# A two-layer attention trunk on one core: the v and gate projections by seven quarter products, and token-major output projections

## The chip, the cores and the metric

The kernel runs on one core of a Trainium2 chip. The metric is the device time of one launch in microseconds (us). The engines are named as in the profile: PE (TensorE, matmuls), PEld (its weight loads), DVE (VectorE), ACT (ScalarE), POOL (GpSimd), SP (SyncE, which issues the DMAs here).

## The reference, cut to what matters

There are 512 tokens of 1024 features and two layers. Both token mixers of a layer read the same normalised input; A has 16 heads of 64 with three dilated patterns, B has 8 differential heads.

```
hdn = rms_norm(x, norm_w)
u = hdn @ w_in                       # 1024 x 10240
qa, ka, va, za, qb, kb, vb, zb, ga, gb = split_cols(u)      # 1024 columns each
ya = dilated_mixture(rope(qa), rope(ka), va) * silu(za)
yb = rms_norm(diff_attention(rope(qb), rope(kb), vb, lam), subln_w) * (1 - lam_init) * silu(zb)
merged = sigmoid(ga) * (ya @ w_proj_a) + sigmoid(gb) * (yb @ w_proj_b)
x = x + merged @ w_out               # after both layers: rms_norm(x, final_norm_w)
```

## The kernel before, in words

**Precision.** Every projection is done as three matmuls of rounded parts: each operand is split into a high part and the rest, and high·high, high·low and low·high are added up in PSUM. The weights come from DRAM in float32 tiles of 128x1024 (`raw`), and for each ACT writes the high part `whi` (L84) and DVE the rest `wlo` (L85).

**Chunks.** A projection of 1024 columns is cut into chunks. `proj_T` makes 256 columns by 512 tokens, feature-major: 48 matmuls of 128x512, weights stationary (L164 to L166). `proj_V` makes 512 tokens by 256 columns, token-major: 96 matmuls of 128x256, the input stationary (L216 to L218). q with k, z, the gates, pa and pb are T chunks, as is layer 0's output projection; v and layer 1's output projection are V chunks.

**Windows.** After a first z, qk and v chunk a layer goes through 17 windows: 8 for the head pairs of branch A, 8 for the heads of branch B and one more. `run` puts the main steps (the chunks' matmuls) and the side steps (a head's scores, softmax, transposes and products with v) of a window in turn. The windows' chunks are qk of the next head, v or z in turn, pa in windows 9 to 12 and the gates in 15 and 16; pb and the output projection follow. `WINDOWS` and `chunk_order` hold that order. A scheduler then fixes one order of instructions for each engine, in which each engine works; buffers of one pool (`blk`, 27 of 4 KB a partition; `tmp`; `wpool` with 3 each of raw, whi and wlo) are taken in turn.

**One head.** The scores `s(layer, branch, head)` go to PSUM; DVE takes the row maximum (L314), ACT the exponential (L315). In branch B, DVE joins the two softmaxes (L408 to L414), PE transposes them to `t` (L332), ACT and DVE split that to `pt` (L333, L334), PE multiplies with v to `o` (L424), and the output is normed (L431 to L443), turned (`ot`, L448), multiplied with the gate path and split to `yb` (L451 to L455). q and k get their rotation on evacuation: a shuffle (L237), products on DVE and POOL (L239, L240), a sum (L241), the split (L248), and DMAs into `qx` and `kx`.

**Input.** `h_block` splits a feature block of x, and `sq_block` squares it on ACT; POOL adds the squares up, and `rstd_cols` sums over the features by 16 matmuls with ones (`ps_ss`, L140). Of the last layer's residual, PE turns x1 to token-major by transposes (`xt`, L564).

Of the kernel before, what the change touches and what calls it, by code (L numbers as in the profile page):

```python
# [12 lines left out]
OP = mybir.AluOpType  # L13
# [19 lines left out]
def trunk_kernel(ctx: ExitStack, tc: tile.TileContext, x, win, wpa, wpb, wout, norm_w, subln_w, final_w, lams,  # L33
                 negb, rope, ident_in, out):
# [3 lines left out]
    blk = ctx.enter_context(tc.tile_pool(name="blk", bufs=27))  # L38
# [22 lines left out]
    halves = [(w, layer, i, h) for layer in range(DEPTH) for w, i in chunk_order() for h in range(2)]  # L61

    def w_src(entry):
        w, layer, i, h = entry
        return {"in": win, "pa": wpa, "pb": wpb, "out": wout}[w][layer, i, h]

    raw, whi, wlo = {}, {}, {}
    n_dma = [0]
    n_split = [0]

    def dma_to(i):
        while n_dma[0] <= min(i, len(halves) - 1):
# [5 lines left out]
    def split_to(i):
        while n_split[0] <= min(i, len(halves) - 1):
            j = n_split[0]  # L80
            dma_to(j)
            whi[j] = wpool.tile([P, 4, 256], F32R, tag="whi", name=f"whi{j}")
            wlo[j] = wpool.tile([P, 4, 256], F32R, tag="wlo", name=f"wlo{j}")
            nc.scalar.activation(whi[j], raw[j], AF.Copy)  # L84
            nc.vector.tensor_tensor(wlo[j], raw.pop(j), bits(whi[j]), OP.subtract)  # L85
            n_split[0] += 1
            dma_to(j + 3)
# [24 lines left out]
    def h_block(layer, m, xt):  # L112

        h = b4(f"h{layer}_{m}")
        nc.scalar.activation(h[:, 0], xt, AF.Copy, scale=nw[:, layer, m:m + 1])
        nc.vector.scalar_tensor_tensor(h[:, 1], xt, nw[:, layer, m:m + 1], bits(h[:, 0]), OP.mult, OP.subtract)  # L116
        st_["hnew"][m] = h

    def sq_block(m, xt):

        s = t2(f"sq{m}")
        nc.scalar.activation(s, xt, AF.Square)  # L122
        if m == 0:
# [9 lines left out]

    def rstd_cols():

        ps = pst.tile([P, T], F32, tag="t", name="ps_ss")
        for n, sq in enumerate((st_["acc"], st_["sq7"])):
            for tb in range(4):
                c = 4 * n + tb
                nc.tensor.matmul(ps[:, c:c + 1], sq[:, tb * P:(tb + 1) * P], ones[:, 0:1], start=True, stop=True)  # L140
# [19 lines left out]
    def mm3(ps, hb, wi, kk, c0, first, last):  # L160

        w_h = whi[wi][:, kk, c0:c0 + P]
        w_l = wlo[wi][:, kk, c0:c0 + P]
        nc.tensor.matmul(ps, w_h, hb[:, 0], start=first, stop=False)  # L164
        nc.tensor.matmul(ps, w_h, hb[:, 1], start=False, stop=False)  # L165
        nc.tensor.matmul(ps, w_l, hb[:, 0], start=False, stop=last)  # L166

    chunk_no = [0]

    def proj_T(rhs, evac, first=False):  # L170
# [635 lines left out]
```

## Time and profile before

| | |
|---|---|
| time of three runs | 1409.91 us median (1409.31 to 1410.14) |
| time of the profiled execution, its span | 1411.3 us, 1409.5 us |
| mean granted TensorE clock | 0.994 of full speed |
| busy: PE, PEld | 1384.4 us (98%), 1197.9 us (85%) |
| busy: DVE, ACT, POOL | 914.5 us (65%), 718.2 us (51%), 317.9 us (23%) |
| DMA queue of the kernel | 180.73 MB, 44.6% of 16 engines' span |

Busy time is the union of an engine's instructions; the matmuls overlap in it, so their cost is read from start to start. The profile's 40 slices show PE at nine tenths or more in all but the first two and the last, so that the end moves with PE's work and with PE's waits.

### The profile page before, as it was taken

The page shows a single profiled execution, that of the slowest core. Times are in us where ns is not written, and L with a number is a line of the kernel's source. Part 1 is how long each engine was busy: PE and PEld are TensorE (multiplying, and loading weights), DVE is VectorE, ACT ScalarE, POOL GpSimd, SP SyncE. Part 2 cuts the span into 40 slices and gives each one's busy share as a digit, 9 for nine tenths or more (in the row PEclk, how much of TensorE's full clock was granted, in tenths as well). Part 3 has the DMA queues.
Part 4 walks back from the last instruction along what each step waited for, and adds up shares of the span by engine and source line. Part 5 has one row for each costly group of instructions (what it writes and reads, how often), then busy time and mean ns, then how long its engine had stood idle before and what let it go on. Part 6 is the DMA issues. An engine that isn't in the chain of part 4 may idle for free.

```text
span 1409.5 us, 21036 instructions
## 1 busy us (share of the span) xinstructions
PE 1384.4 (98%) x7592; PEld 1197.9 (85%) x7592; DVE 914.5 (65%) x1836; ACT 718.2 (51%) x1402; POOL 317.9 (23%) x251
## 2 busy tenths in 40 slices
PE   7899999999999999999989999999999999999998
PEld 6798888988888988888878988989888989888898
DVE  6677777775567775345546777777755778653554
ACT  4456565654455666333434565655544656653333
POOL 3353444400011111110213444444001111111000
PEclk9999999999999999999999999999999999999999
DMA  6464554445535453332544554445535344533521
GB/s 213 125 165 116 140 134 120 120 116 153 151 116 138 121 150 120 105 105 93 186 136 117 138 139 120 120 109 137 144 119 164 105 135 115 148 112 106 163 84 67
DMA packets 67559, 182.07 MB, mean 129 GB/s; under 512 B 9984, under 2 KB 10112, under 8 KB 67456
## 3 DMA queue, kind: packets, MB, share of 16 engines
q1 hardware_dynamic: 67456, 180.73, 44.6%
q8 instruction: 60, 0.98, 0.3%
q14 instruction: 43, 0.35, 0.1%
HBM read 121.97 MB, written 8.39 MB: 92 GB/s over the span
## 4 chain that ended last, share of the span: by engine, by line
PE 95%; DVE 2%; DMA 1%; issue 1%; ACT 1%; SPq 0%; POOL 0%; POOLq 0%; ACTq 0%
PE pj L164 22%; PE pj L165 21%; PE pj L166 21%; PE pv L216 5%; PE pv L218 5%; PE pv L217 5%; DMA x<-x_d 0%; DMA kx(1, 0, 0)0_6921<-hl(1, 0, 0)1_6918 0%; DVE h L116 0%; DVE wlo L85 0%; DMA kx(1, 0, 1)1_7204<-hl(1, 0, 1)1_7197 0%; PE xt L564 0%; PE ps_ss L140 0%; DMA kx(0, 0, 0)0_364<-hl(0, 0, 0)1_361 0%; SPq L232 0%
## 5 line engine op out<-in xcount | busy, mean ns | idle before, releaser
L164 PE MATMUL pj<-h,whi 128*128 128x512 f32 x1024 | 410.0, 402 | 5.9 <-DVE whi L621 5.9
L165 PE MATMUL pj<-h,whi 128*128 128x512 f32 x1024 | 403.2, 394 | 1.2 <-DVE h L116 1.1
L166 PE MATMUL pj<-h,wlo 128*128 128x512 f32 x1024 | 403.0, 395 | 0.1
L85 DVE TENSOR_TENSOR wlo<-raw,whi 128x1024 fp32r<-128x1024 f32 x207 | 276.0, 1334 | 111.7 <-ACT whi L84 108.5
L84 ACT ACTIVATE whi<-raw 128x1024 fp32r<-128x1024 f32 x207 | 218.5, 1056 | 175.9 <-PE pj L165 100.2
L166 PEld LDWEIGHTS pj<-h,wlo 128*128 128x128 f32 x1024 | 192.8, 188 | 41.7 <-DVE wlo L85 0.5
L164 PEld LDWEIGHTS pj<-h,whi 128*128 128x128 f32 x1024 | 193.2, 189 | 39.4 <-issue 5.9
L165 PEld LDWEIGHTS pj<-h,whi 128*128 128x128 f32 x1024 | 193.2, 189 | 34.9 <-DVE h L116 2.9
L216 PE MATMUL pv<-whi,h 128*128 128x256 f32 x512 | 148.5, 290 | 0.0
L218 PE MATMUL pv<-whi,h 128*128 128x256 f32 x512 | 146.5, 286 | 0.0
L217 PE MATMUL pv<-wlo,h 128*128 128x256 f32 x512 | 146.4, 286 | 0.0
L217 PEld LDWEIGHTS pv<-wlo,h 128*128 128x128 f32 x512 | 99.5, 194 | 1.1
L216 PEld LDWEIGHTS pv<-whi,h 128*128 128x128 f32 x512 | 99.4, 194 | 1.0
L218 PEld LDWEIGHTS pv<-whi,h 128*128 128x128 f32 x512 | 99.3, 194 | 0.1
L517 POOL TENSOR_TENSOR g<-g,pr 128x512 f32<-128x512 f32 x16 | 23.7, 1482 | 138.0 <-ACT g L516 105.4
L514 DVE TENSOR_TENSOR g<-pj,rb 128x512 f32<-128x512 f32 x32 | 22.1, 689 | 25.6 <-PE pj L166 25.4
L126 POOL TENSOR_TENSOR sq<-sq,sq 128x512 f32<-128x512 f32 x12 | 18.9, 1575 | 86.4 <-ACT sq L122 86.1
L217 PE MATMUL pv<-wlo,mg 128*128 128x256 f32 x128 | 35.7, 283 | 0.0
L218 PE MATMUL pv<-whi,mg 128*128 128x256 f32 x128 | 35.7, 283 | 0.0
L216 PE MATMUL pv<-whi,mg 128*128 128x256 f32 x128 | 35.4, 283 | 0.0
L525 DVE TENSOR_TENSOR g<-pj,g 128x512 f32<-128x512 f32 x16 | 11.1, 692 | 30.5 <-PE pj L166 30.5
L529 ACT ACTIVATE mg<-g 128x512 fp32r<-128x512 f32 x16 | 10.1, 631 | 29.5 <-DVE g L526 29.5
(4687 smaller groups left out, 2838.3 us busy)
## 6 DMA issues: line engine op xcount, KB each, us to landing
raw<-win_d SPq DMA_DIRECT2D x159, 512.0 KB, 3.6
raw<-wpa_d SPq DMA_DIRECT2D x16, 512.0 KB, 3.6
raw<-wpb_d SPq DMA_DIRECT2D x16, 512.0 KB, 3.5
raw<-wout_d SPq DMA_DIRECT2D x16, 512.0 KB, 3.5
pa_dram<-pa SPq DMA_DIRECT2D x16, 256.0 KB, 2.8
pr<-pa_dram SPq DMA_DIRECT2D x16, 256.0 KB, 3.9
xr<-x_d SPq DMA_DIRECT2D x8, 256.0 KB, 4.8
x_dram<-xr SPq DMA_DIRECT2D x8, 256.0 KB, 2.9
```

The costliest lines, as they stand in the source:

```text
L84: nc.scalar.activation(whi[j], raw[j], AF.Copy)
L85: nc.vector.tensor_tensor(wlo[j], raw.pop(j), bits(whi[j]), OP.subtract)
L126: nc.gpsimd.tensor_tensor(st_["acc"], st_["acc"], s, OP.add)
L164: nc.tensor.matmul(ps, w_h, hb[:, 0], start=first, stop=False)
L165: nc.tensor.matmul(ps, w_h, hb[:, 1], start=False, stop=False)
L166: nc.tensor.matmul(ps, w_l, hb[:, 0], start=False, stop=last)
L216: nc.tensor.matmul(ps, hh, whi[wi][:, k % 4], start=(k == 0), stop=False)
L217: nc.tensor.matmul(ps, hh, wlo[wi][:, k % 4], start=False, stop=False)
L218: nc.tensor.matmul(ps, hl, whi[wi][:, k % 4], start=False, stop=(k == 7))
L514: nc.vector.tensor_tensor(g[:, b], ps, rb, OP.mult)
L517: nc.gpsimd.tensor_tensor(g[:, 0], g[:, 0], st_.pop(("pa", m)), OP.mult)
L525: nc.vector.tensor_tensor(g[:, 1], ps, g[:, 1], OP.mult)
```

## The change

**Seven products.** Each 1024-wide projection of v and of the gates (four in a layer) is made token-major by `proj_S`: the input and the weight are cut in 2x2 quarters, and seven products of sums and differences of quarters (24 matmuls of 128x512 each) take the place of eight. The four sums of the input's quarters (`h_sums`, S1 to S4) are made on DVE and split on ACT and DVE. Four differences of the weight's quarters (`prep_S`: 8 operations of 128x1024 for a projection) are made on POOL; seven operands instead of four quarters are split to `whi` and `wlo`. Three partial results are copied by ACT (`keep`) and added by DVE (`add`).

**Order.** gate 0, v of branch A, gate 1, the first qk and v of branch B stand at the head of a layer. Their results go to DRAM (`g_dram`, `v_dram`); a head loads its v (`vt`), pa and pb their gates. The windows keep qk in each and z in each second one; pa, now token-major by V chunks, stands in windows 15 and 16, two each.

**Projections pb and out** are token-major in two chunks 512 wide (`proj_W`, 96 matmuls of 128x512 over four PSUM banks, the input's feature blocks outside). The results of pb, and of layer 0's out, are turned to feature-major by PE (`turned`), and x1 goes through DRAM.

**Norm.** x comes a second time, token-major (`xtok`), and ACT sums the squares as it makes them; the `ps_ss` matmuls and POOL's sums of squares are gone. `blk` has 30 buffers instead of 27 and holds the S chunks' raw quarters, sums, v and loaded gates as well.

The diff, cut to its core:

```diff
-    blk = ctx.enter_context(tc.tile_pool(name="blk", bufs=27))
+    blk = ctx.enter_context(tc.tile_pool(name="blk", bufs=30))
...
+    def prep_S(j, c, i):
...
+        name = ("11", "21", "T2", "11", "12", "22", "21")[i // 2]
+        flat = q[name, p].rearrange("p a t -> p (a t)") if (name, p) in q else None
+        split(j, flat)
+        if i in (2, 3):
+            nc.gpsimd.tensor_tensor(q["11", p], q["12", p], q["11", p], OP.subtract)
+            q["T2", p] = f4(f"T2_{c}{p}")
+            nc.gpsimd.tensor_tensor(q["T2", p], q["22", p], q["11", p], OP.subtract)
+        elif i in (4, 5):
+            nc.gpsimd.tensor_tensor(q["12", p], q["22", p], q["12", p], OP.subtract)
+        elif i in (6, 7):
+            nc.gpsimd.tensor_tensor(q["21", p], q["21", p], q["T2", p], OP.subtract)
...
+    def square(layer, tb, c, src):
...
+        nc.scalar.activation(scr, src, AF.Square, accum_out=ss[:, c, tb:tb + 1])
...
+    def tok3(ps, hh, hl, wi, o, n, first, last):
+
+        w_h, w_l = whi[wi][:, o:o + n], wlo[wi][:, o:o + n]
+        nc.tensor.matmul(ps, hh, w_h, start=first, stop=False, skip_group_check=True)
+        nc.tensor.matmul(ps, hh, w_l, start=False, stop=False, skip_group_check=True)
+        nc.tensor.matmul(ps, hl, w_h, start=False, stop=last, skip_group_check=True)
...
+    def proj_W(what, lhs, evac):
...
+        for k in range(8):
+            for tb in range(4):
+                steps.append((683, lambda k=k, tb=tb: step(k, tb)))
...
+        def keep(name, ps, a):
+            cp[name, a] = t2(f"{name}_{c}{a}")
+            nc.scalar.activation(cp[name, a], ps, AF.Copy)
+
+        def add(name, ps, a):
+            t = t2(f"o{name}_{c}{a}")
+            nc.vector.tensor_tensor(t, ps, cp.pop((name, a)), OP.add)
+            return t
...
+        for i in range(7):
+            for kk in range(4):
+                for a in range(2):
+                    steps.append((683, lambda i=i, kk=kk, a=a: step(i, kk, a)))
...
+    for tb in range(4):
+        xt = f4(f"xt{tb}")
+        nc.sync.dma_start(xt, xtok[tb])
+        for i in range(2):
+            square(0, tb, i, xt[:, i])
...
-        run(zz(layer, 0, 0, True)())
-        run(chain(qk(layer, 0, 0), vv(layer, 0, 0)))
+        sums = [(0, lambda: h_sums(layer, ("S1", "S2"))), (0, lambda: h_split(layer, ("S2", "S1"))),
+                (0, lambda: h_sums(layer, ("S3", "S4"))), (0, lambda: h_split(layer, ("S3", "S4")))]
+        g = gate(layer, 0)()
+        run(g[:4] + [(0, rstd_cols)] + g[4:8] + sums[:2] + g[8:16] + sums[2:] + g[16:])
+        run([(0, layer_tables)] + vs(layer, 0)())
+        run(gate(layer, 1)())
+        run(qk(layer, 0, 0)())
...
+        run(vs(layer, 1)())
...
-        if s:
-            w[2 * s - 1].append(("v", s // 4, s % 4))
-            w[2 * s].append(("z", s // 4, s % 4))
+        w[2 * s].append(("z", s // 4, s % 4))
     for i in range(4):
-        w[9 + i // 2].insert(1, ("pa", i))
-    for m, i in enumerate((15, 15, 15, 16, 16, 16, 16, 16)):
-        w[i].append(("gate", m))
+        w[15 + i // 2].append(("pa", i))
```

**PE in layer 0, branch-B head 1.** Before, the last two score matmuls of this head, `s(0, 1, 1)13`, are followed by the fourth token block of a v chunk (`pv`, 24 matmuls) and 20 matmuls of a T chunk, with one of the next head's scores between them, and only then by the head's first transposes `t((0, 1, 1), 0)0`; the first of these rows:

```order
L312 MATMUL s(0, 1, 1)13_3640<-kx(0, 1, 1)1_3056,qx(0, 1, 1)_2983 128x512
L313 MATMUL s(0, 1, 1)13_3640<-kx(0, 1, 1)1_3056,qx(0, 1, 1)_2983 128x512
L216 MATMUL pv23_3_3655<-whi46_3424,h0_0_123 128x256
L217 MATMUL pv23_3_3655<-wlo46_3425,h0_0_123 128x256
L218 MATMUL pv23_3_3655<-whi46_3424,h0_0_123 128x256
```

In the change `s(0, 1, 1)13` is followed by 14 products with v of the head before (`o(0, 1, 0)1`), of which these are the last, then by that head's four turns `ot`, eight transposes of this head, its first product with v, and then the next main chunk (`pj`):

```order
L598 MATMUL o(0, 1, 0)1_3960<-vt(0, 1, 0)_3563,pt2_103 128x256 x2
L598 MATMUL o(0, 1, 0)1_3960<-vt(0, 1, 0)_3563,pt1_102 128x256 x2
L622 MATMUL ot(0, 1, 0)_4012<-ident_93,of(0, 1, 0)_3940 128x128 x4
L507 MATMUL t((0, 1, 1), 0)0_4089<-ident_93,p(0, 1, 1)0_3876 128x128
L507 MATMUL t((0, 1, 1), 0)0_4089<-ident_93,p(0, 1, 1)01_3895 128x128
L507 MATMUL t((0, 1, 1), 0)0_4089<-ident_93,p(0, 1, 1)0_3876 128x128 x2
L507 MATMUL t((0, 1, 1), 0)1_4114<-ident_93,p(0, 1, 1)0_3876 128x128
L507 MATMUL t((0, 1, 1), 0)1_4114<-ident_93,p(0, 1, 1)01_3895 128x128
L507 MATMUL t((0, 1, 1), 0)1_4114<-ident_93,p(0, 1, 1)0_3876 128x128 x2
L598 MATMUL o(0, 1, 1)0_4182<-vt(0, 1, 1)_3848,pt0_101 128x256
L251 MATMUL pj21_0_4223<-h0_0_125,whi90_4073 128x512
```

The main matmuls that stood between a head's last score and its transposes now stand behind its first product with v.

**DVE at the same place.** In the change, between the head's join of the softmaxes (L588) and the first split of its transposes (`pt0`, L509), DVE has the norm of the head before (`rs`, `of`), its `yf` and `yb`, and the first rope steps (`sw`, `rot`) of two finished q and k chunks:

```order
L588 SCALAR_TENSOR_TENSOR p(0, 1, 1)0_3876<-p(0, 1, 1)1_3989,rq(0, 1, 1)_4039,p(0, 1, 1)0_3876 128x512
L210 TENSOR_SCALAR rs(0, 1, 0)_3941<-rs(0, 1, 0)_3941 128x4
L615 TENSOR_TENSOR rs(0, 1, 0)_3941<-rs(0, 1, 0)_3941,rb(0, 1, 0)_3810 128x4
L617 TENSOR_TENSOR of(0, 1, 0)_3940<-of(0, 1, 0)_3940,rs(0, 1, 0)_3941 128x512
L625 SCALAR_TENSOR_TENSOR yf(0, 1, 0)_4017<-ot(0, 1, 0)_4012,subw_215,z(0, 1, 0)_3771 128x512
L393 STREAM_SHUFFLE sw(0, 1, 2)1_4050<-pj19_1_3948 128x512
L395 TENSOR_TENSOR rot(0, 1, 2)1_4052<-pj19_1_3948,ct_96 128x512
L393 STREAM_SHUFFLE sw(0, 1, 3)0_4124<-pj20_0_4079 128x512
L395 TENSOR_TENSOR rot(0, 1, 3)0_4126<-pj20_0_4079,ct_96 128x512
L629 TENSOR_TENSOR yb(0, 1, 0)_4019<-yf(0, 1, 0)_4017,yb(0, 1, 0)_4019 128x512
L509 TENSOR_TENSOR pt0_101<-t((0, 1, 1), 0)0_4089,pt0_101 128x512
```

PE's product `o(0, 1, 1)0` needs `pt0`, the last of these rows, so that all of them now stand ahead of the next main chunk.

**ACT at the start of the program.** In the change the third of the seven products needs the split sum `S2_00`. Ahead of it ACT has the eight squares of the token-major x (`scr`) and, between them, the splits of a weight difference (`T2_01`) and of `raw0`, which POOL has overwritten with a difference by then:

```order
L219 ACTIVATE scr000_187,ss0_186<-xt0_184 128x512
L219 ACTIVATE scr001_189,ss0_186<-xt0_184 128x512
L101 ACTIVATE whi5_289<-T2_01_178 128x1024
L101 ACTIVATE whi6_336<-raw0_107 128x1024
L219 ACTIVATE scr010_193,ss0_186<-xt1_191 128x512
```

Five more squares follow, and then, behind the last of them, two copies of partial results (`c`) and the splits of the sums:

```order
L219 ACTIVATE scr031_207,ss0_186<-xt3_203 128x512
L339 ACTIVATE c1_00_243<-X0_0_216 128x512
L339 ACTIVATE c1_01_248<-X0_1_220 128x512
L205 ACTIVATE S2_00_258<-S2f00_254 128x512
L205 ACTIVATE S2_01_261<-S2f01_256 128x512
```

Before, the same place holds x's splits and squares of a feature-major x (`h`, `sq`) and the split of the second weight tile:

```order
L115 ACTIVATE h0_2_133<-x0_1_111,nw_89 128x512
L122 ACTIVATE sq0_136<-x0_0_106 128x512
L115 ACTIVATE h0_3_138<-x0_1_111,nw_89 128x512
L84 ACTIVATE whi1_141<-raw1_113 128x1024
L122 ACTIVATE sq1_151<-x0_0_106 128x512
```

The second load of x and POOL's weight differences now stand ahead of PE's third product.

## Rows read from the trace of the kernel before

**Rows 1.** Page, busy time of each engine, then the chain by engine.

```profile
PE 1384.4 (98%) x7592; PEld 1197.9 (85%) x7592; DVE 914.5 (65%) x1836; ACT 718.2 (51%) x1402; POOL 317.9 (23%) x251
...
PE 95%; DVE 2%; DMA 1%; issue 1%; ACT 1%; SPq 0%; POOL 0%; POOLq 0%; ACTq 0%
```

**Rows 2.** PE's waits: tile, line, releaser; us in total, times, longest.

```profile
PE pj L164 <- DVE whi L621: 5.9, 1, 5.9
PE s(1, 0, 0)00_7068 L307 <- DMA kx(1, 0, 0)0_6921<-hl(1, 0, 0)1_6918: 5.6, 1, 5.6
PE s(0, 0, 0)00_526 L307 <- DMA kx(0, 0, 0)0_364<-hl(0, 0, 0)1_361: 5.1, 1, 5.1
...
PE s(1, 0, 1)00_7225 L307 <- DMA kx(1, 0, 1)1_7204<-hl(1, 0, 1)1_7197: 0.9, 1, 0.9
```

**Rows 3.** Timeline of PE in layer 0's output projection; start, duration.

```profile
663.21 0.39 PE L164 MATMUL pj<-mg,whi 128*128 128x512 f32 x1
...
664.57 0.39 PE L164 MATMUL pj<-mg,whi 128*128 128x512 f32 x1
```

**Rows 4.** Timeline of PE in layer 1's output projection.

```profile
1356.93 0.28 PE L216 MATMUL pv<-whi,mg 128*128 128x256 f32 x1
...
1357.88 0.28 PE L218 MATMUL pv<-whi,mg 128*128 128x256 f32 x1
```

**Rows 5.** Timeline of PE where four transposes interrupt it.

```profile
1352.81 0.39 PE L166 MATMUL pj<-yb(1, 1, 2)_10928,wlo 128*128 128x512 f32 x1
1353.04 0.60 PE L564 MATMUL xt<-ident,xr 128*128 128x128 f32 x4
...
1353.71 0.40 PE L165 MATMUL pj<-yb(1, 1, 3)_11239,whi 128*128 128x512 f32 x1
```

**Rows 6.** Chain in order of time: start, us, what.

```profile
24.52 1.68 PE ps_ss L140 x16
```

**Rows 7.** Windows: busy us (instructions) by engine, PEclk, DMA.

```profile
50.00:60.00 10.00, 10.00 (x49) 9.07 (x48) 4.59 (x12) 4.89 (x11) 0.03 (x1) 0.79 0.34 102
455.00:483.00 28.00, 28.00 (x173) 24.94 (x173) 22.38 (x54) 19.27 (x43) 3.59 (x3) 1.00 0.47 132
740.00:750.00 10.00, 8.92 (x41) 8.44 (x42) 3.87 (x8) 3.47 (x7) 0.00 (x0) 0.66 0.22 65
```

**Rows 8.** Timeline of DVE, layer 0, a branch-A window.

```profile
108.14 1.23 DVE L85 TENSOR_TENSOR wlo<-raw,whi 128x1024 fp32r<-128x1024 f32 x1 [1.18 <-ACT whi L84]
...
110.84 0.75 DVE L237 STREAM_SHUFFLE sw(0, 0, 3)1_1141<-pj 128x512 f32<-128x512 f32 x1
111.47 0.68 DVE L239 TENSOR_TENSOR rot(0, 0, 3)1_1143<-pj,ct 128x512 f32<-128x512 f32 x1
112.06 2.05 DVE L85 TENSOR_TENSOR wlo<-raw,whi 128x1024 fp32r<-128x1024 f32 x1
```

**Rows 9.** Timeline of POOL in the same stretch.

```profile
111.73 1.30 POOL L240 TENSOR_TENSOR sw(0, 0, 3)1_1141<-sw(0, 0, 3)1_1141,st 128x512 f32<-128x512 f32 x1 [6.01 <-DVE sw(0, 0, 3)1_1141 L237]
```

**Rows 10.** POOL and ACT groups by shape: busy us, mean ns, idle.

```profile
L126 POOL TENSOR_TENSOR sq<-sq,sq 128x512 f32<-128x512 f32 x12 | 18.9, 1575 | 86.4 <-ACT sq L122 86.1
...
L122 ACT ACTIVATE sq<-x 128x512 f32<-128x512 f32 x8 | 4.7, 615 | 0.0
```

**Rows 11.** Timeline, layer 0, branch-B head 1: softmax end.

```profile
351.14 0.69 DVE L314 CUSTOM_DVE_ANT_0 p(0, 1, 1)13_3641<-s(0, 1, 1)13_3640,nbt 128x512 f32<-128x512 f32 x1 [2.37 <-PE s(0, 1, 1)13_3640 L313]
...
354.39 0.75 DVE L414 SCALAR_TENSOR_TENSOR p(0, 1, 1)03_3441<-p(0, 1, 1)13_3641,rq(0, 1, 1)_3647,p(0, 1, 1)03_3441 128x512 f32<-128x512 f32 x1
```

**Rows 12.** Timeline of the same head: output, norm, mult.

```profile
385.39 0.38 ACT L431 ACTIVATE of(0, 1, 1)_3888<-o(0, 1, 1)1_3939 128x256 f32<-128x256 f32 x1 [2.81 <-PE o(0, 1, 1)1_3939 L424]
...
387.74 1.01 POOL L132 TENSOR_TENSOR rs(0, 1, 1)_3889<-rs(0, 1, 1)_3889,mhalf 128x4 f32<-128x4 f32 x1 [19.59 <-DVE rs(0, 1, 1)_3889 L131]
...
389.01 0.69 DVE L443 TENSOR_TENSOR of(0, 1, 1)_3888<-of(0, 1, 1)_3888,rs(0, 1, 1)_3889 128x512 f32<-128x512 f32 x1
```

**Rows 13.** DMA of the first 20 us, in slices of half a microsecond.

```profile
GB/s 0 0 0 15 91 225 361 320 295 266 274 246 258 303 295 332 406 381 385 393 393 410 422 414 430 377 372 385 407 401 385 378 418 402 401 410 262 139 33 0
```

More of the change, by code (lines that the diff above doesn't have):

```diff
@@ L78, in split_to @@
[L78 to L87, printed above, removed]
+    chunks, loads = plan()
@@ new lines, in trunk_kernel @@
+    preps, need, first_prep, first_load = [], [], [], []
+    n = 0
+    for c, ch in enumerate(chunks):
+        first_prep.append(len(preps))
+        first_load.append(n)
+        if ch[0] == "S":
+            preps += [(c, i) for i in range(14)]
+            need += [n + k for k in (1, 2, 6, 8)] + [n + 8] * 10
+            n += 8
+        else:
+            m = 4 if ch[0] == "W" else 2
+            preps += [(c, i) for i in range(m)]
+            need += [n + i + 1 for i in range(m)]
+            n += m
@@ new lines, in prep_to, with next_chunk @@
+    def prep_to(i):
+        while n_prep[0] <= min(i, len(preps) - 1):
+            j = n_prep[0]
+            c, k = preps[j]
+            load_to(need[j])
+            if chunks[c][0] == "S":
+                prep_S(j, c, k)
+            else:
+                split(j, raw.pop(first_load[c] + k))
+            n_prep[0] += 1
+            load_to(need[min(j + 3, len(need) - 1)])
+    chunk_no = [0]
+    def next_chunk(what):
+        c = chunk_no[0]
+        chunk_no[0] += 1
+        assert chunks[c][1] == what, (chunks[c], what)
+        return c, first_prep[c]
@@ L132, in inv_sqrt, with layer_tables @@
         nc.gpsimd.tensor_tensor(r, r, mhalf, OP.pow)
-    def rstd_cols():
[L136 to L140, printed above, removed]
+    def square(layer, tb, c, src):
+        if "ss" not in st_:
+            st_["ss"] = small.tile([P, 2, 4], F32, tag="ssum", name=f"ss{layer}", bufs=2)
+        ss = st_["ss"]
+        scr = tmp.tile([P, T], F32, tag="t2", name=f"scr{layer}{tb}{c}")
+        nc.scalar.activation(scr, src, AF.Square, accum_out=ss[:, c, tb:tb + 1])
+    def rstd_cols():
+        ss = st_.pop("ss")
         r = small.tile([P, 4], F32, tag="rstd", name="rstd", bufs=2)
-        nc.vector.tensor_copy(r, ps[:, 0:4])
-        nc.vector.tensor_tensor(r, r, ps[:, 4:8], OP.add)
+        nc.vector.tensor_tensor(r, ss[:, 0], ss[:, 1], OP.add)
         inv_sqrt(r, r, 1.0 / D, 1e-6)
         st_["rcol"] = r
-    def rstd_rows():
+    def layer_tables():
         ps = pst.tile([P, T], F32, tag="t", name="ps_rb")
@@ L157, in layer_tables, with proj_T @@
         nc.gpsimd.tensor_tensor(st, rb, st, OP.mult)
[L160 to L170, printed above, removed]
+    def proj_T(what, rhs, evac):
         steps = []
-        c = chunk_no[0]
-        chunk_no[0] += 1
-        i0 = 2 * c
+        c, j0 = next_chunk(what)
         hold = {}
@@ new lines, in ev, with turn, turns @@
+        def ev(tb, ps):
+            nc.vector.tensor_tensor(r[tb], ps, r[tb], OP.add)
+            nc.sync.dma_start(x1_dram[tb, :, i], r[tb])
+            square(layer + 1, tb, i, r[tb])
+        def turn(j):
+            h_block(layer + 1, 4 * i + j, turned(f"xt{layer}{i}{j}", lambda tb: r[tb][:, j * P:(j + 1) * P]))
+        def turns():
+            return [(300, lambda j=j: turn(j)) for j in range(4)]
+        main = lambda: [(0, pre)] + proj_W((layer, "out", i), lambda k: st_["mg", k], ev)
```

528 lines of the change are left out of this document (309 added, 219 removed).

## Prediction

> **What bounds the kernel now.** I read the page first: PE is busy for 98% of the span and holds 95% of the chain that ended last; DVE stands at 65%, ACT at 51%, POOL at 23% [rows 1]. So PE's work counts in full, and another engine counts only where PE waits for it. PE's waits come next: 5.9 us at the start, and 5.6, 5.1 and 0.9 us for the first scores, which wait for the DMAs that fill `kx` [rows 2]. Behind the long ones the granted clock is below 1: 0.79 in the ten microseconds after the first, 0.66 around the second, which costs 2.1 + 3.4 = 5.5 us in these two stretches [rows 7]. A branch-B window such as 455 to 483 us has PE busy throughout, and DVE for 22.4 of 28 us, or 80% [rows 7]: PE has a fifth to spare before DVE is the bound, and this only while DVE's work may lie anywhere in the window.
>
> **What the change takes from PE.** A matmul's price is read from start to start. Six steps of 128x512 take 664.57 - 663.21 = 1.36 us, 0.2267 each [rows 3]; eight of 128x256 take 0.95 us, 0.119 each [rows 4]. By the order, 4032 main matmuls of 512 become 4416, and 1920 of 256 become 768: 384 x 0.2267 - 1152 x 0.119 = 87.1 - 137.1 = **-50.0 us**. Transposes go from 8 groups of four to 24. One group stretches two steps (1352.81 to 1353.71) from 0.45 to 0.90 us, so it costs 0.45 [rows 5]; sixteen more are **+7.2**. The sums by `ps_ss`, 1.68 us in each layer [rows 6], go: **-3.4**. PE's own work thus falls by 46.2 us. The first scores now come behind a whole v product of 168 matmuls, 38 us, which hides the DMAs into `kx`: I take away the three waits, **-11.6**, and the low clock behind them, **-5.5**. All this is -63.3 us. From here on come the waits that the change makes.
>
> **The start: +23.** PE's first two products (48 matmuls, 10.9 us) need only x and raw weights. The third needs `S2_00`, in front of which ACT has eight squares of the second copy of x and the splits of weight differences that POOL must make first. By the order of SP, the fifth weight tile, which POOL's first difference needs, is behind 4.7 MB, and the four tiles of that copy behind 9.5 to 11.1 MB. The first 8 us moved some 1.6 MB, and from there on about 0.39 MB per us came in [rows 13]: the fifth tile lands at 8 + 3.1 / 0.39 = 16 us, the copy of x at 28 to 32. POOL's operations are twice as wide as the 1.30 us one [rows 9]: 2.6 each, and `T2_01` is the sixth: 16 + 15.6, it is there at about 32. Then come its split, that of `raw0`, six squares of 0.615 [rows 10], two copies and `S2`: the third product starts near 42 us, with 10.9 us of PE work done, a lag of 31. In the kernel before, PE lags some 11 us (5.9 of them its first wait). I add 21 and 2 for a low clock behind the wait. Bounds: 11, if only POOL's sixth difference holds it, and 28, if POOL's 1.58 us under DVE's load [rows 10] holds.
>
> **The quarter products elsewhere: +11.** One has 38.1 us of PE work (168 x 0.2267). Against it stand 14 DVE splits of 1.22 (one alone is 1.23 [rows 8]), 17.1 us, and 8 POOL differences, 20.6 us; in sequence they would be 37.7. I count less than 1 us for each of six passages from one to the next, **+5**, and **+6** for layer 1's first, whose sums, `h` blocks and weight differences come together. Bounds: 0 and 25.
>
> **The windows.** The v chunks, gates and pa leave the windows that they filled, while the heads' side work stays. By the order and the rows' durations, the branch-A windows of a layer now hold 194 us of PE work and about 164 of DVE (85%); I add 0.6 us for each of 14 windows, **+8** (bounds 0 and 20). Branch B's windows 1 to 6 hold 155 us of PE and 145 of DVE, with the odd ones above PE: 24.6 us of PE against 29.0 of DVE in the first, 23.2 against 25.5 in the third, 24.2 against 27.4 in the fifth, and 22.3 against 19.3 in the even ones between. The order makes it worse: before, 44 main matmuls, about 7.4 us, lie between a head's last score and its transposes; now only 14 products with v (14 x 0.119 = 1.7 us), four turns (0.45) and eight transposes (0.9), 3.05 us. What DVE and ACT must do meanwhile I add up along the rows shown: row maximum, exponential and join 4.0 us (351.14 to 355.14 [rows 11]); the last part of the norm, with POOL's power of 1.01, 2.0 us (387.74 to 389.70 [rows 12]); the turns 0.45; then on DVE `yf`, about 0.75 like the join's widest operation, two shuffles and two products 2 x (0.75 + 0.68) [rows 8], `yb` and `pt0` 0.69 each, as the 0.69 of a 512-wide product [rows 12]. With 0.4 us before the maximum this is 12.2 us; less 3.05, PE stands for some **9 us**. Heads 1, 3 and 5 have this order in both layers: 6 x 9 = **+54**. Bounds: DVE's surplus alone, 3.3 us a head, is 20; with the smaller gaps that I see at heads 0 and 6 (2.5 and 5.5 us a layer) it is 70. After a pause of 5.1 us the clock was 0.79 [rows 2, 7]; for pauses that scores and products break up I count 1.3 us each, **+8** (0 to 20).
>
> **The end: +4.** The four token blocks of the last chunk now finish together, and DVE has four times the sum, the product with the final weight and the scaling of 512 columns one after another, where before each block's tail lay beside the next one's matmuls. Bounds 0 and 6.
>
> **At nothing** I put the new DMAs and ACT's copies. The DMA engines' share is 0.47 in the B window [rows 7]; a head's `vt` is asked for with its first scores, a window's length before its use, and the gates of pb behind a chunk of 96 x 0.2267 = 22 us; were that cover gone, each would cost a wait like the 5 us on `kx` [rows 2]. ACT has 51% of the span [rows 1].
>
> **Sum.** -63.3 + 23 + 11 + 8 + 54 + 8 + 4 = +44.7 us against the profiled execution's 1411.3, that is 1456. That execution lies 1.4 us above the median of the runs, so I say **1455**.
>
> **A rule against the change.** The split at 108.14 takes 1.23 us alone; the one at 112.06, of the same size, takes 2.05 [rows 8], and POOL's product runs from 111.73 to 113.03 [rows 9], 0.97 us of it beside the split: DVE loses 0.82 of them, nearly all. The weight differences are POOL operations of the same kind, 64 of 2.6 us. In the Trainium skill, SBUF — State Buffer, section "Who interferes with whom" says that a DVE instruction with two SBUF inputs contends with a GpSimd one that reads SBUF, through a shared read interface. The trace agrees, by 0.82 of 0.97 us. By it, 20.6 us of POOL differences and 17.1 of splits in a quarter product would hardly overlap; the sum by that is the first rival's, and by the durations alone the forecast's.
>
> **Rivals.**
> *The ports bind the quarter products, 1485.* By rows 8 and 9 a split hardly moves while POOL works. With the gate's or v's evacuation beside 37.7 us of splits and differences, a v product needs about 42 us of DVE instead of 38.1, and the first of a layer 55: 4 + 4 + 17 us a layer, less the 11 and part of the start that are counted: +30. For it: rows 8 and 9; against it: PSUM-sided operations (the product of 0.68 at 111.47) keep their time. Chance 0.15.
> *The windows absorb everything, 1385.* PE stays the bound, as it is in every window now, and the pauses do not come: 1411.3 - 63.3 + 23 + 11 + 4 = 1386. For it: 98% of PE today; against it: the order at heads 1, 3, 5. It decides at 26 us of pauses in all windows, 4.3 us for each of the six heads instead of 9: below that the change is faster. Chance 0.15.
> *Only DVE's surplus counts, 1408.* The pauses are as long as DVE's work exceeds PE's in odd windows, 10 us a layer (4.4 + 2.3 + 3.2), and even windows give nothing back: 1386 + 20, with 2 for the clock. For it: DVE would use its even windows to run ahead; against it: `pt` cannot be made ahead of the transposes. Chance 0.15.
>
> **How the numbers follow.** The forecast has 0.55, with a range of its own from 1430 to 1480. What a measurement can tell from no change is 0.2%, 2.8 us. Faster: 0.15, half of the third rival, 0.07, rounded to 0.22; same 0.05; slower 0.73. The range of 1388 to 1488 leaves out some 0.10 of the second rival below, and above it 0.06 of the first and 0.04 for pauses at the upper bound.
>
> **What would show it.** PE's first `S2` product starting near 42 us; PE waits at `t` and `o` of branch B's heads 1, 3, 5 in both layers, some 9 us each, released by DVE; no wait on `kx`; branch-B windows longer than 29 us with DVE near 90%; splits of 2 us in the first 150 us of each layer. I am wrong if PE is still at 98% there, or if the first 200 us hold the loss.

## The result and the profile after

The changed kernel takes 1511.7 us (1509.5 to 1513.69, 4 runs) against 1409.61 us for the kernel before, a ratio of 1.073 with an interval of 1.071 to 1.074: 102 us slower. I had forecast 1455 and a range of 1388 to 1488. The profiled execution took 1513.69 us, its span 1511.9 at a mean granted clock of 0.961.

The page of the changed kernel first: engines, and PE's busy tenths and clock in 40 slices.

```profile
PE 1382.4 (91%) x6856; PEld 1154.0 (76%) x6856; DVE 1067.4 (71%) x1927; ACT 776.1 (51%) x1468; POOL 463.9 (31%) x287
...
PE   4898899999998898999989898999999988989996
...
PEclk8899999999999998999989899999999999989999
```

PE is busy for as long as before (1384.4 us [rows 1]) with 46 us less work in it, so part of that time is at a low clock, and it now stands for 9% of the span. The dips lie in slices 1 to 5, 13 to 16, 21 to 25 and 33 to 36, of 37.8 us each: twice in each layer. To date them I cut the span at the first scores of each branch, the first matmul of pb, the head of layer 1 and so on. The view by windows (columns as in [rows 7]):

```profile
7.00:42.60 35.60, 15.75 (x48) 9.81 (x48) 28.45 (x29) 17.53 (x33) 22.64 (x8) 0.74 0.69 268
42.60:228.60 186.00, 169.12 (x701) 136.05 (x702) 136.34 (x130) 96.54 (x122) 76.84 (x29) 0.94 0.46 152
228.60:427.00 198.40, 196.41 (x997) 165.75 (x996) 157.26 (x347) 121.32 (x246) 99.21 (x78) 1.00 0.60 161
427.00:665.80 238.80, 215.26 (x1248) 187.57 (x1249) 168.89 (x406) 126.36 (x300) 29.41 (x25) 0.96 0.50 140
665.80:760.00 94.20, 93.63 (x438) 76.81 (x436) 49.48 (x57) 27.51 (x37) 8.04 (x4) 1.00 0.61 212
760.00:967.40 207.40, 185.89 (x765) 148.51 (x766) 152.65 (x139) 107.75 (x140) 95.78 (x34) 0.93 0.42 141
967.40:1165.80 198.40, 196.38 (x997) 165.73 (x996) 157.28 (x347) 121.30 (x246) 99.10 (x78) 1.00 0.59 160
1165.80:1404.00 238.20, 213.47 (x1211) 184.01 (x1212) 167.87 (x402) 125.60 (x299) 28.33 (x24) 0.95 0.51 138
```

| stretch | length | PE's work, at 0.2267 and 0.119 a step | excess | forecast |
|---|---|---|---|---|
| start to the third product | 42.6 us | 10.9 | 31.7 | 31 |
| rest of the quarter products, the first qk and 24 matmuls of the first window, layer 0 | 186.0 | 157.8 | 28.2 | about 4 |
| the same in layer 1, all of it | 207.4 | 168.7 | 38.7 | about 9 |
| branch-A windows, idle, each layer | 198.4 | | 2.0 | 4 |
| branch B to pb, idle and low clock, each layer | 238.8, 238.2 | | about 33 | 31 |

PE does the 24 matmuls ahead of the first scores (696 and 744 of 128x512 in all); the expectation of experiment 1 was written without them and so has 33 and 44 for 28 and 39. The idle part of the branch-B line is 238.8 - 215.3 = 23.5 us in layer 0, and PE's busy 215 us at a clock of 0.96 lose some 9 more (an estimate). So all terms came out near their size but one: the heads of the layers, where the quarter products stand. PE's waits:

```profile
PE X L266 <- ACT whi L101: 13.2, 5, 6.9
PE Y L266 <- DVE h L177: 10.2, 2, 7.3
PE X L266 <- ACT S L205: 10.1, 1, 10.1
PE Y L267 <- DVE wlo L102: 9.8, 2, 7.2
PE X L266 <- DVE v L433: 8.9, 2, 4.4
PE X L267 <- DVE wlo L102: 8.7, 6, 3.4
PE ot(1, 1, 0)_10571 L622 <- DVE of(1, 1, 0)_10499 L617: 6.4, 1, 6.4
...
PE ot(0, 1, 0)_4012 L622 <- DVE of(0, 1, 0)_3940 L617: 5.2, 1, 5.2
```

The six waits at `ot`, of which two are shown, are the pauses of branch B (5.6 us on average). Above them stand waits of quarter products (`X`, `Y`) for splits, for the evacuation of v and for the input's blocks; the one of 10.1 us is the start's. What makes these late shows in one stretch of layer 0, first DVE, then POOL:

```profile
89.78 2.29 DVE L102 TENSOR_TENSOR wlo<-T,whi 128x1024 fp32r<-128x1024 f32 x1 [3.33 <-ACT whi L101]
91.99 3.38 DVE L102 TENSOR_TENSOR wlo<-raw,whi 128x1024 fp32r<-128x1024 f32 x1
95.96 1.21 DVE L102 TENSOR_TENSOR wlo<-raw,whi 128x1024 fp32r<-128x1024 f32 x1
```

```profile
88.62 2.36 POOL L125 TENSOR_TENSOR raw<-raw,raw 128x1024 f32<-128x1024 f32 x1
90.94 3.35 POOL L127 TENSOR_TENSOR raw<-raw,T 128x1024 f32<-128x1024 f32 x1
```

A split takes 1.21 us at 95.96, when POOL is idle, and 2.29 and 3.38 us beside the differences. A difference with no such operation of DVE's beside it takes 2.40:

```profile
165.06 2.40 POOL L121 TENSOR_TENSOR raw<-raw,raw 128x1024 f32<-128x1024 f32 x1 [25.75 <-DVE wlo L102]
```

The two engines take turns. The split at 89.78 starts while POOL works; POOL ends at 90.98, the split 1.09 us later. POOL's next, at 90.94, starts within that split and ends 2.22 us after it, at 94.29; the split at 91.99 starts within that one and ends 1.08 us after it. So it is throughout: 47 splits of this execution start during a `TENSOR_TENSOR` of POOL's, and 46 end 1.08 to 1.15 us after it (the other runs at full speed, in a row of DVE operations beside which POOL's takes 5.62 us); 26 differences start during a split, and all end 2.20 to 2.57 us after it. A 128x64 product that DVE makes between two others grows too, and so do all 64 differences:

```profile
177.91 2.41 DVE L821 CUSTOM_DVE_ANT_0 lam_s<-lam_t 128x64 f32<-128x64 f32 x1
188.63 0.21 DVE L821 CUSTOM_DVE_ANT_0 lam_s<-lam_t 128x64 f32<-128x64 f32 x1
```

```profile
L127 POOL TENSOR_TENSOR raw<-raw,T 128x1024 f32<-128x1024 f32 x16 | 48.3, 3025 | 1.2 <-DVE lam_e L821 1.2
...
L125 POOL TENSOR_TENSOR raw<-raw,raw 128x1024 f32<-128x1024 f32 x16 | 43.9, 2745 | 0.5
```

The small product takes 2.41 us with POOL at work and 0.21 without; the differences take 2.75 to 3.03 on average. DVE's operations that read PSUM keep their times, as the 0.68 in [rows 8] had: 32 sums of a PSUM result and a copy (L343) take 0.68 on average. An operation need not have two inputs in SBUF to suffer: layer 1's casts of the input's blocks, with one, take 0.79 us on average here and 0.42 without differences (in experiment 1, where the line is L169):

```profile
L177 DVE CAST h<-hf 128x512 fp32r<-128x512 f32 x8 | 6.1, 788 | 6.8 <-ACT hf L175 6.8
L169 DVE CAST h<-hf 128x512 fp32r<-128x512 f32 x8 | 3.2, 424 | 7.0 <-ACT hf L167 7.0
```

### The profile page after: what moved, and what is told of

The parts are those of the page before. It is cut to its first block, busy times and chain, and to the rows that moved or that the text cites. A ratio compares the mean times of both kernels' runs of the same rounds, so it can differ in the third digit from the quotient of the medians.

```text
span 1511.9 us, 20024 instructions
## 1 busy us (share of the span) xinstructions
PE 1382.4 (91%) x6856; PEld 1154.0 (76%) x6856; DVE 1067.4 (71%) x1927; ACT 776.1 (51%) x1468; POOL 463.9 (31%) x287
## 5 line engine op out<-in xcount | busy, mean ns | idle before, releaser
L102 DVE TENSOR_TENSOR wlo<-raw,whi 128x1024 fp32r<-128x1024 f32 x240 | 332.1, 1385 | 167.3 <-ACT whi L101 166.8
L251 PE MATMUL pj<-h,whi 128*128 128x512 f32 x768 | 305.6, 398 | 0.0
L252 PE MATMUL pj<-h,whi 128*128 128x512 f32 x768 | 305.5, 398 | 0.0
L253 PE MATMUL pj<-h,wlo 128*128 128x512 f32 x768 | 303.5, 396 | 0.0
L251 PEld LDWEIGHTS pj<-h,whi 128*128 128x128 f32 x768 | 145.7, 190 | 27.0
L252 PEld LDWEIGHTS pj<-h,whi 128*128 128x128 f32 x768 | 145.6, 190 | 26.8
L266 PE MATMUL X<-whi,h 128*128 128x512 f32 x128 | 49.9, 414 | 15.9 <-DVE v L433 8.9
L266 PE MATMUL X<-whi,S 128*128 128x512 f32 x128 | 49.0, 421 | 16.5 <-ACT S L205 10.1
L267 PE MATMUL X<-wlo,S 128*128 128x512 f32 x128 | 54.6, 429 | 8.9 <-DVE wlo L102 8.7
L268 PE MATMUL X<-whi,S 128*128 128x512 f32 x128 | 53.3, 422 | 0.0
L267 PE MATMUL X<-wlo,h 128*128 128x512 f32 x128 | 52.0, 408 | 0.0
L268 PE MATMUL X<-whi,h 128*128 128x512 f32 x128 | 51.1, 405 | 0.1
L266 PE MATMUL pw<-whi,mg 128*128 128x512 f32 x128 | 50.9, 400 | 0.0
L267 PE MATMUL Y<-wlo,S 128*128 128x512 f32 x128 | 50.2, 392 | 0.0
L127 POOL TENSOR_TENSOR raw<-raw,T 128x1024 f32<-128x1024 f32 x16 | 48.3, 3025 | 1.2 <-DVE lam_e L821 1.2
L268 PE MATMUL pw<-whi,mg 128*128 128x512 f32 x128 | 47.8, 393 | 0.0
```

The source lines that it names most:

```text
L102: nc.vector.tensor_tensor(wlo[j], src, bits(whi[j]), OP.subtract)
L127: nc.gpsimd.tensor_tensor(q["21", p], q["21", p], q["T2", p], OP.subtract)
L251: nc.tensor.matmul(ps, w_h, hb[:, 0], start=(k == 0), stop=False)
L253: nc.tensor.matmul(ps, w_l, hb[:, 0], start=False, stop=(k == 7))
L266: nc.tensor.matmul(ps, hh, w_h, start=first, stop=False, skip_group_check=True)
L267: nc.tensor.matmul(ps, hh, w_l, start=False, stop=False, skip_group_check=True)
```

## The experiments

All of them are changes of the changed kernel. A time without a range is that of one execution; beside these the kernel before took 1408.8 to 1409.2 us. The first four were to tell apart a theory of ports (DVE and POOL hold each other up), one of order (splits, evacuations and three weight buffers in a fixed order make the waits), and, for branch B, one of cover (PE lacks main work in the odd windows).

**1. No differences.** The quarters are split and multiplied raw; this leaves out part of the computation.

```diff
-        name = ("11", "21", "T2", "11", "12", "22", "21")[i // 2]
+        name = ("11", "21", "12", "11", "12", "22", "21")[i // 2]
...
-            nc.gpsimd.tensor_tensor(q["11", p], q["12", p], q["11", p], OP.subtract)
```

(and the other three `nc.gpsimd` lines of `prep_S`)

> The changed kernel without POOL's 64 weight differences: raw quarters are split and multiplied in their place, so the v and gate products are not the reference's; loads, splits, matmuls and sums stay. Theory A (ports): DVE operations with two SBUF inputs and POOL's differences hold each other up, and this is what stretches the stages of quarter products; in the changed kernel layer 0's stage ends 33 us and layer 1's 44 us later than PE's work from the third product on. Without the differences some 10 us of each should be left, and the time falls by about 60 to 1450; a split should take 1.23 us in these stages. Theory B (order): splits, evacuations and three weight buffers in a fixed order make the waits, whatever POOL does; then only a few us at the start go, and the time stays above 1495.

1453.25 us. The third product starts at 34.5 us instead of 42.7, the first scores come at 195.8 instead of 228.6, and layer 1's head, from its first product to its first scores, takes 175.0 us instead of 206.6. The split's row:

```profile
L102 DVE TENSOR_TENSOR wlo<-raw,whi 128x1024 fp32r<-128x1024 f32 x256 | 324.1, 1267 | 195.1 <-ACT whi L101 186.8 <-DMA m<-g_dram 4.3 <-PE pj L245 1.2
```

The mean is 1.27 us; in the changed kernel 240 such splits take 332.1 us and the 16 of `T2` 35.4, a mean of 1.44. POOL's differences cost 58 us in all. Order and the three weight buffers are as before and cost little by themselves: layer 0's second, third and fourth quarter products take PE's own pace, and 3.5 us (layer 0) and 6.3 (layer 1) of the heads' excess are left. First these three stretches here, then in the changed kernel:

```profile
63.90:102.30 38.40, 38.37 (x168) 31.45 (x168) 24.73 (x26) 22.97 (x28) 0.00 (x0) 1.00 0.53 183
103.20:141.50 38.30, 38.30 (x169) 31.73 (x170) 21.41 (x21) 22.14 (x27) 0.00 (x0) 1.00 0.56 202
152.30:190.50 38.20, 38.20 (x170) 31.65 (x169) 29.05 (x44) 24.43 (x30) 1.29 (x1) 1.00 0.42 117
```

```profile
73.10:117.60 44.50, 40.85 (x168) 32.44 (x168) 32.89 (x26) 22.87 (x28) 24.09 (x9) 0.96 0.46 158
122.00:162.00 40.00, 39.99 (x169) 32.80 (x170) 26.13 (x21) 21.32 (x26) 17.31 (x6) 0.96 0.53 179
172.80:223.30 50.50, 41.83 (x170) 32.84 (x169) 41.63 (x45) 24.56 (x31) 17.65 (x7) 0.90 0.30 83
```

**2. The differences on DVE.** `nc.gpsimd` becomes `nc.vector` in the four lines.

> The changed kernel with the 64 weight differences on DVE instead of POOL (the result stays the reference's). Theory A (ports): DVE gets 64 x 1.23 = 79 us of work but nothing blocks it, a quarter product then has 17 us of splits, 10 of differences and 7 of evacuations, less than PE's 38: about 1470. Theory B (order): DVE's in-order queue is longer in the same stages, and the time rises above 1515.

1473.74 us, 38 less than with POOL, although DVE has 64 x 1.22 = 78 us more to do. Its busy time even falls, from 1067.4 us to 1060.4, since part of the former was waiting for its turn (some 85 us, an estimate: 1067.4 + 78 - 1060.4):

```profile
PE 1376.4 (94%) x6856; PEld 1154.8 (78%) x6856; DVE 1060.4 (72%) x1991; ACT 779.1 (53%) x1468; POOL 282.1 (19%) x223
...
L121 DVE TENSOR_TENSOR raw<-raw,raw 128x1024 f32<-128x1024 f32 x16 | 19.5, 1221 | 0.2
```

**3. Eight products.** Gates and v by two `proj_W` chunks each.

```diff
-        return lambda: proj_S((layer, "v", br), ev_v(layer, br))
+        e = ev_v(layer, br)
+        return lambda: chain(*[lambda h=h: proj_W((layer, "v", br, h), hrhs, lambda tb, ps: e(tb, h, ps)) for h in range(2)])
...
```

(the gates likewise, and the list of loads)

> v and gates by eight products (two 512-wide chunks of 96 matmuls for each projection) at the same place, token-major, through DRAM as in the change; no sums, no differences, eight splits for 14 (the result stays the reference's). PE's work rises by 8 x 24 x 0.2267 = 43.5 us. Theory A (ports): the waits of both stages (about 77 us with the start's 23 partly in it) go for the most part, so about 1470: seven products cost more than they save. Theory B (order and the head of the layer): the waits stay, and the time is near 1540.

1470.81 us. The first scores come at 194.5 us with 185 us of PE work before them, and the quarter products' waits are gone from PE's list. Seven products save 43.5 us of matmuls and lose 84 to waits and the low clock. Of the 62 us that are left over the kernel before, branch B's v in its windows takes 52 away (experiment 7).

**4. pa earlier.**

```diff
-        w[15 + i // 2].append(("pa", i))
+        w[9 + 2 * i].append(("pa", i))
```

> The changed kernel with one line changed: the four pa chunks stand in windows 9, 11, 13 and 15 (one each) instead of two each in 15 and 16 (the result stays the reference's). Theory C: PE pauses at branch-B heads 1, 3, 5 because the odd windows hold only one chunk of main work, 10.9 us; with 11.4 us more the pauses of some 5 to 6 us at each turn (33 us a layer with the low clock and smaller gaps) go for the most part: about 1455, with no wait of over 2 us at ot. Rival: DVE's work itself binds branch B (145 us of DVE against 155 of PE), so that pauses only move: 1490 or more.

1504.69 us: the rival's number. The waits at `ot` of heads 0, 2 and 4 are gone, and others stand in their place: six behind DVE's evacuation of pa, and one a layer at the last head, which pa no longer covers.

```profile
PE pv L266 <- DVE pg L685: 11.1, 6, 2.6
...
PE ot(0, 1, 7)_6033 L622 <- DVE of(0, 1, 7)_6000 L617: 4.1, 1, 4.1
PE ot(1, 1, 7)_12592 L622 <- DVE of(1, 1, 7)_12559 L617: 4.1, 1, 4.1
```

pa in the odd windows did cover the pauses that it was put at; the gain was given back. So the next experiment used work that is evacuated by ACT and DVE in short steps and that left these windows with the change, and let pa stay.

**5. Branch B's v back in its windows** (7, 9, 11, 13), in 256-wide chunks, through DRAM.

```diff
     for i in range(4):
+        w[7 + 2 * i].append(("vb", i))
         w[15 + i // 2].append(("pa", i))
...
-        run(vs(layer, 1)())
...
```

> The changed kernel with one projection put back: v of branch B is made by four 256-wide chunks in windows 7, 9, 11 and 13, as before the change, and no quarter product of it stands at the head of a layer (v still goes through DRAM; the result stays the reference's). The pauses at branch B come from the missing main work, and what replaces it must not wait for DVE's queue as pa did. Theory C (cover): the pauses and the low clock behind them go, some 60 us; the waits of that quarter product go, 18 us in layer 0 and 10 in layer 1; PE does 2 x 7.6 us more: 1512 - 60 - 28 + 15 = about 1440, and no wait at ot over 2 us. Rival (DVE binds branch B): the pauses move again as they did with pa, and only the quarter product's waits go: 1490 or more.

1448.56 us; no wait at `ot` is left, and PE's idle time from layer 0's first branch-B scores to its last turn falls from 25.5 us to 1.9. Cover was what the branch-B windows lacked, in a form that does not wait for DVE's queue. The 63 us hold the waits of one quarter product a layer as well; experiment 7 has the cover without them.

**6. The same, the remaining differences on DVE.**

> The same with the remaining 48 weight differences on DVE instead of POOL (the result stays the reference's). If ports and cover add up: 1474 for the differences on DVE, less 60 for the pauses, less some 5 of waits, plus 15 of PE work, about 1424. If the one hides the other, 1440 or more.

1416.8 us: the two effects add up. PE's clock in the first 50 us is still 0.80, with 20.8 us idle there.

**7. Experiments 3 and 5 together.**

> Eight products for the gates and branch A's v (512-wide chunks at the head of a layer), branch B's v back in windows 7, 9, 11 and 13; DRAM for v, gates and x1, and 512-wide pb and output projections as in the change (the result stays the reference's). PE's work by the rows of before: 4224 x 0.2267 + 1536 x 0.119 = 1140 us of main matmuls, 2 less than before the change, 7 more of transposes, 3 less of sums; the waits for kx are hidden (17 with the low clock). Cover theory: no quarter products, no pauses: 1411 + 2 - 17 + 4 at the end + 9 in the branch-A windows = about 1410, level with the kernel before (1405 to 1420). Rival: the other parts of the change (DRAM, 512 wide) have a cost of their own: 1440 or more.

1418.39 us (1417.31 to 1423.14), 1.0077 times the kernel before (1.0056 to 1.0097): all other parts of the change together (DRAM, the turns, the 512-wide projections, the norm) cost some 9 us over that kernel, the quarter products and the empty windows the rest.

**8. POOL at work that nobody reads.** Experiment 1 with 64 additions of 128x1024 on POOL; `q` is a raw quarter, `idle` a tile of its own, and `blk` has 29 buffers instead of 30, here and in 9. This too leaves out the differences.

```diff
...
+            nc.gpsimd.tensor_tensor(idle, q[name, p], q[name, p], OP.add)
```

> The kernel without weight differences (raw quarters in their place, 1453 us), to which 64 additions of 128x1024 on POOL are given back whose result nothing reads: each adds a raw quarter to itself into a tile of its own, at the place of the differences; blk has 29 buffers. It tells two forms of the port theory apart. Lock: POOL's work itself holds up DVE's operations with two SBUF inputs; DVE's surplus under POOL returns to some 70 us and the time to 1485 to 1510. Latency: what cost was that splits and PE had to wait for POOL's slow results; nobody waits here, and the time stays at 1450 to 1462.

1468.99 us, between the two: 16 us over experiment 1.

**9. The same with two quarters.** Now it reads two tiles, as a difference does.

```diff
+        pairs = {2: (("12", "11"), ("22", "11")), 4: (("22", "12"),), 6: (("21", "22"),)}
+        for x, y in pairs.get(i - p, ()):
+            nc.gpsimd.tensor_tensor(idle, q[x, p], q[y, p], OP.subtract)
```

> As the kernel with 64 unread additions on POOL (1469 us), but each unread operation subtracts two different raw quarters, the same pairs as the changed kernel's differences. If the kind of POOL's read mattered, DVE's surplus under POOL rises from 42 us towards the 72 of the changed kernel and the time to 1485 or more: then the lock is most of the cost. If it stays within 6 us of 1469, the lock alone is worth some 16 us, and the rest of the 59 us that go with POOL's differences comes from waiting for their results.

1491.01 us, 38 over experiment 1. The rows of the split and of POOL in experiment 8, then in 9, each with the shortest, median and longest of POOL's operations in ns:

```profile
L102 DVE TENSOR_TENSOR wlo<-raw,whi 128x1024 fp32r<-128x1024 f32 x256 | 370.4, 1450 | 156.7 <-ACT whi L101 153.6 <-DMA raw<-ws_d 1.9 <-DMA kx(1, 0, 3)0_8713<-hl(1, 0, 3)1_8710 0.3
L121 POOL TENSOR_TENSOR idle<-raw 128x1024 f32<-128x1024 f32 x64 | 164.4, 2569 | 185.4 <-DMA raw<-ws_d 181.5
L121 POOL TENSOR_TENSOR idle<-raw x64: 1892/2754/7055, 5.8 to 865.8; 128x1024 f32<-128x1024 f32 x64
```

```profile
L102 DVE TENSOR_TENSOR wlo<-raw,whi 128x1024 fp32r<-128x1024 f32 x256 | 387.5, 1521 | 154.5 <-ACT whi L101 152.7 <-PE pj L249 1.2
L122 POOL TENSOR_TENSOR idle<-raw,raw 128x1024 f32<-128x1024 f32 x64 | 196.1, 3064 | 186.4 <-DMA raw<-ws_d 141.1 <-issue 40.4 <-POOL st L231 0.7
L122 POOL TENSOR_TENSOR idle<-raw,raw x64: 2345/3256/7360, 16.8 to 893.9; 128x1024 f32<-128x1024 f32 x64
```

Beside experiment 1's 324.1 us DVE's splits take 46 and 63 us more. POOL's operation takes 1.89 us undisturbed where it reads one tile twice and 2.35 to 2.40 where it reads two; beside DVE both grow, to a median of 2.75 and 3.26. Work on POOL that nothing waits for thus costs 38 of the 58 us. The other 20 lie in branch B's v: its products take 50.5 and 47.5 us in the changed kernel, 38.2 in experiment 1, and 38.2 in 9, where POOL has done its unread operations by then. Whether waiting for POOL's results makes these 20, or only meeting DVE's work at another time, no run tells.

**10. A first projection that needs no difference.** Experiment 6 with gate 0 of layer 0 by eight products, its sums of the input's quarters further back, and then that of layer 1 too. The edit of the second (the first has `if layer == 0 and which == 0`):

```diff
+        if which == 0:
+            return lambda: chain(*[lambda h=h: proj_W((layer, "gate", 0, h), hrhs, lambda tb, ps: e(tb, h, ps)) for h in range(2)])
         return lambda: proj_S((layer, "gate", which), e)
...
```

> As with the differences on DVE and branch B's v in the windows (1417), but the first projection of the program, gate 0 of layer 0, by eight products (two 512-wide chunks), so that PE has 43.5 us of work that needs no weight difference and no sum while the second x and the sums come in; 40 differences are left, on DVE. PE does 5.4 us more; the third product's wait, 6.4 us of it on S and some on h, and the low clock of the first 50 us (0.80) go, 15 to 20: about 1404, faster than the kernel before (1409). Rival: the quarter products' first sums are late wherever they stand, and the wait moves to branch A's v: 1415 or more.

1408.23 us (1404.47 to 1411.65), a ratio of 0.9993 (0.9984 to 1.0003): no difference from the kernel before, and 8.6 us less than experiment 6's one execution, where I had expected 13.

> As the mixed kernel that ran level with the kernel before (1408), with layer 1's first projection by eight products too, 32 differences left, on DVE. PE does 5.4 us more; layer 1's first waits (about 9 us on h, whi and S) and the low clock there (3.5) go: about 1402, faster than before. Rival: h and x1 of layer 1 are late for any first product, the waits stay at the next projection: 1410 or more.

1404.63 us (1402.83 to 1405.89), a ratio of 0.997 (0.9958 to 0.9982): faster than both kernels, by 4 us and 107 us. Four quarter products are left, which take 96 x 0.2267 = 21.8 us from PE's work of experiment 7; 13.8 of them are gained. PE is busy for 98% again:

```profile
PE 1366.8 (98%) x7336; PEld 1172.7 (84%) x7336; DVE 987.1 (70%) x1927; ACT 739.6 (53%) x1436; POOL 271.2 (19%) x223
```

## Why the prediction was wrong

**The step that failed** is "the quarter products elsewhere: +11", with its bounds of 0 and 25. Behind the third product, layer 0's head lost 28.2 us and layer 1's 38.7, 67 together, where 13 were set with the low clock. I had set 17.1 us of splits and 20.6 of differences in sequence against PE's 38.1 and found them even. In sequence is what the trace shows, at 1.22 and 2.40 us each. What the sum left out is the rest of DVE's work, which stands in the same queue: evacuations, sums and the rotation of q and k. Experiment 1 has DVE's work in a product without differences; eight of 2.40 us on top of it, 19.2, one after the other, give what the products took (an estimate, since the work of one product reaches into the next):

| quarter product, layers 0 and 1 | DVE in experiment 1 | with 19.2 | took |
|---|---|---|---|
| v of branch A | 24.7, 24.7 | 43.9, 43.9 | 44.5, 44.9 |
| gate 1 | 21.4, 21.5 | 40.6, 40.7 | 40.0, 41.7 |
| v of branch B | 29.1, 28.2 | 48.3, 47.4 | 50.5, 47.5 |

PE needs 38.1 for each. Part of that rest is held up as the splits are: 24 of the 32 second halves of v (L433) read SBUF alone and take 0.97 us on average, and 0.75 without the differences. Three weight buffers hold about 8 us of matmuls (36 of them), less than four differences take; whether more buffers would help was not tried. The prediction's own sign of being wrong, a loss in the first 200 us, came in part: the start and layer 0's head hold some 49 us of the loss, 28 of them in this term.

**The first rival** named the mechanism and had 0.15 of the chance; its price, +30 over the forecast, was about half of the 58 us that experiment 1 shows. It counted some 42 us of DVE for a v product and 55 for the first of a layer; layer 1's first took 52.1 from first to last matmul, and the other v products 44.5 to 50.5. The row for it lay in [rows 8, 9], and the Trainium skill, SBUF — State Buffer, section "Who interferes with whom", has a DVE instruction with two SBUF inputs contend with a GpSimd one that reads SBUF; I gave the forecast to the durations alone. That section of the Trainium skill also calls the shared pair of ports "an exclusive lock". The trace agrees: whichever operation starts second ends nearly its whole time after the first, a split 1.08 to 1.15 us of its 1.22, a difference 2.20 to 2.57 (median 2.25) of its 2.40. By the same reading the split at 112.06 in [rows 8] ends 1.08 us after POOL's product of [rows 9].

**The start** (+23) was right in each link: the first squares at 28.1 us (forecast: 28), the split of `T2_01` at 33.5 (32), `S2` at 42.0, the third product at 42.66 (42).

```profile
28.11 0.63 ACT L219 ACTIVATE scr<-xt 128x512 f32<-128x512 f32 x1 [4.42 <-DMA xt<-xtok_d]
...
33.48 1.06 ACT L101 ACTIVATE whi<-T 128x1024 fp32r<-128x1024 f32 x1 [4.04 <-POOL T L123]
...
41.98 1.23 ACT L205 ACTIVATE S<-S2f 128x512 fp32r<-128x512 f32 x2 [1.86 <-DVE S2f L194]
```

**Branch B** (+54 and +8) came out at about 66 us, for a reason that is partly another, and the nearness is in part luck: the six pauses are 33.5 us instead of 54, the low clock some 18 instead of 8, and waits that I had not counted some 15. The chain of 12 us was too long (its terms add up to 11.8 and not 12.2, besides): the last part of it, `yf` to `pt0`'s low half on DVE, is not waited for, since the first product with v needs only the high half, which ACT makes. What stands ahead of the prediction, and the prediction, both had it that the product waits for all those DVE rows. The timeline of PE:

```profile
467.60 1.81 PE L598 MATMUL o(0, 1, 0)1_3960<-vt(0, 1, 0)_3563,pt 128*128 128x256 f32 x14
474.63 1.11 PE L622 MATMUL ot(0, 1, 0)_4012<-ident,of(0, 1, 0)_3940 128*128 128x128 f32 x4 [5.22 <-DVE of(0, 1, 0)_3940 L617]
...
477.73 0.43 PE L598 MATMUL o(0, 1, 1)0_4182<-vt(0, 1, 1)_3848,pt 128*128 128x256 f32 x1
478.01 0.40 PE L251 MATMUL pj<-h,whi 128*128 128x512 f32 x1
```

PE's product at 477.73 starts when ACT's half is done, ahead of DVE's `yb` and `pt0`. The pause is 5.2 us here instead of 9. Experiments 4, 5 and 7 show the cause as forecast (missing main work): with cover PE works through. The third rival, pauses of 10 us a layer by DVE's surplus alone, falls short of the 23.5 and 24.7 us of idle time; experiment 5 does not test it by itself, since v's chunks take that surplus away as well. The forecast's sign of DVE near 90% in these windows did not come: DVE is busy for 168.9 of 238.8 us, 71%.

**The rest.** The waits for `kx` at the first scores of a layer are gone, and two of 2.0 us stand at branch B's first. (Before, the one in layer 1 shows in the slices too: the 21st has PE at eight tenths, which what stands ahead of the prediction passes over.) The end grew from 6.4 us behind the last matmul to 11.6, near the +4 of the forecast. At these sizes the terms add up to some 99 us; between the two spans lie 102.4.

## What to carry to other kernels

Before trading matmuls for elementwise work, give each engine's whole work in the new stage, evacuations too, and add up as one sum what two engines do by turns: here 43.5 us of matmuls were bought with 64 POOL operations that took 58 us back. Where main work is moved out of a window, what it covered must be named; here one projection put back in four windows was worth 52 us (1470.81 to 1418.39), and 63 with the waits of a quarter product (1511.7 to 1448.56). A product that needs nothing prepared belongs first in a stage: that was worth 8.6 us in layer 0, and 3.6 more in layer 1 (experiment 10).

## What I had not expected

That the two engines take turns so strictly. POOL's operation that reads one tile twice takes 1.89 us undisturbed, and cost DVE's splits 46 us and the kernel 16; one that reads two takes 2.40, and cost them 63 and the kernel 38. And DVE, with 78 us more work, was the better place for the differences (1473.74 against 1511.7 us), as the theory of ports had it but not the prediction.
